# A gated decoder step on one core: longer rows for the activations, and matmuls in passes instead of turns

## The chip, the cores and the metric

The kernel runs on one core of a Trainium2 chip. The metric is the device time of one execution in microseconds. The kernel before was timed three times: 1818.37, 1818.59 and 1819.75 us, median 1818.59. A further execution was taken by the hardware profiler; all rows of profiles below come from such executions. "Before" and "after" are the two kernels.

## What is computed

The reference is one layer of a hybrid decoder for 336 tokens (16 learned meta tokens, 256 of a prompt, 8 sequences of 8), with a model width of 2048. Cut to what matters:

```python
h = rms_norm(x, norm_w)
proj = h @ w_in                       # 2048 -> z | x,B,C | dt | short-conv b,c,h,z | gates a,b
xbc = silu(causal_dwconv(xbc) + b)    # width 4
y, state = ssd_chunked(xs, dt, log_a, bm, cm, state, chunk)
y = gated_group_rms_norm(y + d_skip * xs, z, ssd_norm_w)
y_a = y @ w_ssd_out                   # 4096 -> 2048
u = sc_c * sc_h
y_b = (sc_b * causal_dwconv(u) * silu(sc_z)) @ w_sconv_out
merged = sigmoid(g_a) * y_a + sigmoid(g_b) * y_b
out = rms_norm(x + merged @ w_o, final_norm_w)
```

Nearly all arithmetic is in the matrix products: `w_in` has 176.5 blocks of 128 columns, and the three output products have 64 more of the same size.

## The kernel before, in words

Tokens lie along the free dimension and model channels along the 128 partitions. An activation such as the normalized h is a tile of 16 rows (k = 0 to 15) per partition, each row holding the tokens of one block of 128 channels. A product of 128 output channels is then 16 steps over k: a weight tile of 128x128 is loaded into TensorE and a row of up to 336 tokens is streamed past it, and all steps add up in one PSUM bank.

Accuracy comes from a split. Every operand is kept as a high part (rounded to the float32r type) and a low part (the remainder), and three of the four partial products are added: high weight by high activation, high by low, low by high. The activations' parts are `hhi` and `hlo` (both in the tile `hx`), `vhi` and `vlo` for the short-conv branch, `yh` and `yl` for the SSD branch, and, in the first 80 us, before the norm is known, `uhi` and `ulo`.

`wblk` (lines 92 to 99) brings 1024 columns of weights, that is eight k, by a DMA on SP's queue into `wraw`; ACT copies it to the high part `whi` (L96), and DVE subtracts to get the low part `wlo` (L98). `wraw`, `whi` and `wlo` have three buffers each. `unit` (lines 119 to 124) does two such halves for a product of 2048 channels, each with one call of `mm` (lines 110 to 117), which is where the matmuls are issued: 8 k per call, and in the SSD output (`out_units`) 4 k per call. `proj` is `unit` on h, from token t0 on: t0 is 0 for the x and B channels of the SSD (336 columns), 12 for the C channels and for the short conv's c and h (324), and 16 for the rest (320). The matmuls of dt (L340, L341) and those of the last two blocks of the final product have loops of their own.

A row of `hx` is 352 floats long (TS, 1408 bytes), of which 336 are used; rows of `vhi` and `vlo` are 320 floats (1280 bytes), rows of `yh` and `yl` likewise, and rows of `uhi` and `ulo` 336 floats (1344 bytes).

The order of instructions on each engine is that of the program text, except for a few placed by hand after a named instruction and the SSD's steps, which are woven between the projections of the next group (`weave`). What may run when is set by semaphores that a framework places.

Of the kernel before, what the change touches and what calls it, by code (L numbers as in the profile page):

```python
# [8 lines left out]
F32R = mybir.dt.float32r  # L9
# [3 lines left out]

P = 128
T = 336
TS = 352
META = 16
TC = 12
TV = T - META
DM = 2048  # L20
KT = DM // P
# [28 lines left out]
def tile_hybrid_step(ctx, tc, xT, w0, w1, w2, wdt, wso, wsc, wo, cmask, vec, hvec, convst, sconvst, xe_, fwe, h0T,  # L50
                     yA, yB, yE, convo, ssmp, ssms, sconvo):
    nc = tc.nc
# [19 lines left out]
    xk = xT[:, KT:].rearrange("p (k t) -> p k t", t=T)  # L72
    hx = keep.tile([P, 2, KT, TS], F32R, name="hx")[:, :, :, :T]
    hhi, hlo = hx[:, 0], hx[:, 1]
# [15 lines left out]
    latest = {}  # L90
# [17 lines left out]
                                                                         mybir.DependencyReason.DATA), reason="step")  # L108

    def mm(out, hi, lo, xh, xl, base, nk, k0, first, last):  # L110
        for k in range(nk):
            w = hi[:, base + k * P:base + k * P + P]
            nc.tensor.matmul(out, w, xh(k0 + k), start=first and k == 0, stop=False)  # L113
            nc.tensor.matmul(out, w, xl(k0 + k), start=False, stop=False)  # L114
        for k in range(nk):
            w = lo[:, base + k * P:base + k * P + P]
            latest["pe"] = nc.tensor.matmul(out, w, xh(k0 + k), start=False, stop=last and k == nk - 1).ins  # L117

    def unit(src, xh, xl, n):
        pt = ps.tile([P, 512], F32, name="pj")  # L120
        for half in range(2):
            hi, lo = wblk(src[:, half * 1024:half * 1024 + 1024])
            mm(pt[:, :n], hi, lo, xh, xl, 0, 8, half * 8, half == 0, half == 1)
        return pt[:, :n]
# [47 lines left out]
    with tc.tile_pool(name="pa", bufs=2) as pa:  # L172
# [33 lines left out]
        for k in range(KT):  # L206
            split = nc.scalar.activation(uhi[:, k, :], ya[:, k, :], AF.Copy, scale=yan[:, k:k + 1])
            rest = nc.vector.scalar_tensor_tensor(ulo[:, k, :], ya[:, k, :], yan[:, k:k + 1], fb(uhi[:, k, :]), mult, sub)
            if k % 2 == 0:
                hi = wp.tile([P, 1024], F32R, name="whi")  # L210
                lo = wp.tile([P, 1024], F32R, name="wlo")
# [6 lines left out]
            for i, t0 in enumerate((TC, TC, META)):  # L218
                o = 384 * (k % 2) + i * P
                for j, (w, x) in enumerate(((hi, uhi), (hi, ulo), (lo, uhi))):  # L220
                    nc.tensor.matmul(pu[i][:, :T - t0], w[:, o:o + P], x[:, k, t0:],  # L221
                                     start=k == 0 and j == 0, stop=k == 15 and j == 2)
# [86 lines left out]
            nc.vector.tensor_tensor(up[:, :258], up[:, :258], rs2[:, 14:272], mult)  # L309
            nc.vector.tensor_tensor(ups[:, :, 2:10], ups[:, :, 2:10], eights(rs2[:, 272:]), mult)  # L310

        vhi = pa.tile([P, KT, TV], F32R, name="vhi", bufs=1)
        vlo = pa.tile([P, KT, TV], F32R, name="vlo", bufs=1)
        for j in range(KT):
            u = ((up0, ups0), (up1, ups1), u2)[j] if j < 3 else conv_in(j, proj)
            if j == 3:
# [133 lines left out]
    with tc.tile_pool(name="pb", bufs=2) as pb:  # L450
# [285 lines left out]
        def out_units(g, st):  # L736
            yh, yl = st["y"]
            for mp in range(8):
                hi, lo = wblk(wso[g, mp])
                for i in range(2):  # L740
                    m = 2 * mp + i
                    pp = ps.tile([P, 512], F32, name="pj")
                    mm(pp[:, :TV], hi, lo, lambda k: yh[:, k, :], lambda k: yl[:, k, :], 512 * i, 4, 0, True, True)
                    if g == 0:
                        nc.scalar.activation(ya[:, m, :TV], pp[:, :TV], AF.Copy)
                    else:
                        nc.vector.tensor_tensor(ya[:, m, :TV], ya[:, m, :TV], pp[:, :TV], add)  # L747
                yield
# [59 lines left out]
    with tc.tile_pool(name="pc", bufs=3) as pc_:  # L808
# [42 lines left out]
        for m in range(KE, KT):  # L851
# [3 lines left out]
            for half in range(2):  # L855
# [6 lines left out]
                for wide in ((True, False), (False, True))[half]:  # L862
                    for k in range(8):
                        w, x = (h, hx[:, :, 8 * half + k, :NA]) if wide else (l, hhi[:, 8 * half + k, :NA])
                        nc.tensor.matmul(po[:, :(1 + wide) * NA], w[:, k * P:k * P + P], x,  # L865
                                         start=half + k == 0 and wide, stop=half == 1 and k == 7 and wide)
# [20 lines left out]
        def tokens(a, b):  # L887
            for k in range(a, b):
                x = hx[:, :, k, NA:TV]
                for j, (h, w) in enumerate(((0, eh), (1, eh), (0, el))):  # L890
                    nc.tensor.matmul(pt_, x[:, h, :], w[:, :, k * P:k * P + P], start=k == 0 and j == 0,  # L891
                                     stop=k == KT - 1 and j == 2)
            return nc.cur_bb.bb.instructions[-1]

        first = tokens(0, 4)
# [12 lines left out]
        last = tokens(9, KT)  # L908
# [97 lines left out]
def _build(shapes):  # L1006
    import concourse.bacc as _bacc
    import concourse.tile as _tile

    nc = _bacc.Bacc("TRN2", target_bir_lowering=False, num_devices=1, dynamic_dma_scratch_size=8192)  # L1010
    args = [nc.dram_tensor(n, s, F32, kind="ExternalInput").ap() for n, s in shapes]
    args += [nc.dram_tensor(n, s, F32, kind="ExternalOutput").ap() for n, s in _OUTS]
    with _tile.TileContext(nc) as tc:
        tile_hybrid_step(tc, *args)
    return nc
# [23 lines left out]
```

## Time and profile before

| | before |
|---|---|
| median of three runs (lowest to highest) | 1818.59 us (1818.37 to 1819.75) |
| the profiled execution, its own time | 1817.73 us |
| its span, first to last instruction | 1815.9 us |
| mean granted TensorE clock | 0.999 |
| PE busy | 1808.9 us (100%) |
| DVE busy | 1149.1 us (63%) |
| ACT busy | 830.0 us (46%) |
| POOL busy | 389.7 us (21%) |
| HBM read, written | 296.34 MB, 32.88 MB (181 GB/s) |

PE is TensorE's matmuls, PEld its weight loads, which run beside the matmuls. A matmul lasts some 310 ns from its start to its modelled end, but the next one starts long before that end, so PE reads as busy all the time however dense the matmuls are. What tells how fast they follow each other is the distance between two starts. In the rows, "L117" is a line of the kernel, `pj<-hx,wlo` says that the PSUM tile pj is written from the tiles hx and wlo, and `128x320` is the form of the streamed operand. A group's row ends with its busy time in us, the mean duration of one in ns, and the idle time of its engine before it.

### The profile page before, as it was taken

Reading aid. Unit: us, or ns where it says so; the run is one execution under the profiler, and the core shown is the slowest. Engines: PE = TensorE matmul, PEld = TensorE weight load, DVE = VectorE, ACT = ScalarE, POOL = GpSimd, SP = SyncE. Lnnn points to the kernel's source line nnn. Section 1 sums busy time; section 2 is a strip of 40 time slices with the busy share of each in tenths; the row PEclk is TensorE's granted clock in tenths of the full one; section 3 lists DMA queues with packets and bytes.
Section 4 is the critical chain, followed back from the end, with each engine's and each line's share of the span. In section 5 each row is a group of like instructions: output and inputs, shape, how many; then the busy total and the mean of one; then the engine's idle time right before and its main releaser. Section 6 shows DMA issues by size and latency. Waiting matters only on the chain.

```text
span 1815.9 us, 32410 instructions
## 1 busy us (share of the span) xinstructions
PE 1808.9 (100%) x13006; PEld 1792.9 (99%) x13006; DVE 1149.1 (63%) x1696; ACT 830.0 (46%) x1269; POOL 389.7 (21%) x398
## 2 busy tenths in 40 slices
PE   9999999999999999999999999999999999999998
PEld 9999999999999999999999999999999999999998
DVE  7845544454643335658587786877878778676534
ACT  6433333333333334546655354564546556343543
POOL 0100000000000001243253432524334252400012
PEclk9999999999999999999999999999999999999999
DMA  7444444444444446457566574665746657576553
GB/s 257 144 151 149 148 149 148 151 150 149 154 155 160 161 160 229 151 174 237 169 205 228 172 246 154 209 218 181 247 152 216 205 171 251 157 245 214 181 174 127
DMA packets 117286, 331.33 MB, mean 182 GB/s; under 512 B 20944, under 2 KB 37904, under 8 KB 117136
## 3 DMA queue, kind: packets, MB, share of 16 engines
q1 hardware_dynamic: 116272, 327.89, 55.8%
q8 instruction: 102, 1.67, 0.4%
q10 hardware_dynamic: 864, 1.38, 0.2%
q14 instruction: 48, 0.39, 0.1%
HBM read 296.34 MB, written 32.88 MB: 181 GB/s over the span
## 4 chain that ended last, share of the span: by engine, by line
PE 99%; DMA 0%; issue 0%; DVE 0%; POOLq 0%; POOL 0%; ACT 0%; DVEq 0%
PE pj L113 31%; PE pj L114 31%; PE pj L117 31%; PE yb L653 2%; PE ms L639 1%; PE pj L221 1%; PE yb L588 1%; PE ms L537 1%; PE pj L865 1%; PE ms L221 0%; PE yb L716 0%; PE yb L891 0%; PE ms L540 0%; DMA yan<-xT 0%; PE ms L539 0%; PE pj L340 0%
## 5 line engine op out<-in xcount | busy, mean ns | idle before, releaser
L113 PE MATMUL pj<-hx,whi 128*128 128x320 f32 (+2 forms) x2880 | 860.9, 311 | 0.0
L114 PE MATMUL pj<-hx,whi 128*128 128x320 f32 (+2 forms) x2880 | 856.7, 310 | 0.0
L98 DVE TENSOR_TENSOR wlo<-wraw,whi 128x1024 fp32r<-128x1024 f32 x470 | 599.2, 1275 | 404.7 <-PE pj L117 204.1
L96 ACT ACTIVATE whi<-wraw 128x1024 fp32r<-128x1024 f32 x470 | 496.9, 1058 | 756.7 <-PE pj L114 624.0
L113 PEld LDWEIGHTS pj<-hx,whi 128*128 128x128 f32 x2880 | 540.7, 188 | 4.6 <-ACT pad L465 1.7
L114 PEld LDWEIGHTS pj<-hx,whi 128*128 128x128 f32 x2880 | 540.9, 188 | 0.1
L117 PE MATMUL pj<-hx,wlo 128*128 128x320 f32 (+2 forms) x2880 | 484.6, 310 | 0.0
L117 PEld LDWEIGHTS pj<-hx,wlo 128*128 128x128 f32 x2880 | 440.4, 188 | 0.0
L113 PE MATMUL pj<-yh,whi 128*128 128x320 f32 x512 | 153.1, 311 | 0.0
L114 PE MATMUL pj<-yl,whi 128*128 128x320 f32 x512 | 152.1, 308 | 0.0
L599 POOL TENSOR_TENSOR h<-h,decS 128x512 f32<-128x512 f32 x64 | 76.5, 1230 | 147.4 <-PE ms L639 147.4
L244 POOL COPY SCS<-up 128x2 f32<-128x2 f32 x16 | 21.0, 1310 | 358.3 <-DVE up L238 328.2
L113 PEld LDWEIGHTS pj<-yh,whi 128*128 128x128 f32 x512 | 96.0, 188 | 1.2 <-issue 0.2
L114 PEld LDWEIGHTS pj<-yl,whi 128*128 128x128 f32 x512 | 96.0, 188 | 0.6
L117 PE MATMUL pj<-yh,wlo 128*128 128x320 f32 x512 | 95.8, 309 | 0.0
L747 DVE TENSOR_TENSOR yan<-yan,pj 128x320 f32<-128x320 f32 x112 | 54.2, 485 | 62.6 <-PE pj L117 61.3
L474 DVE SCALAR_TENSOR_TENSOR cacc<-pad,V,cacc 128x360 f32<-128x360 f32 (+1 forms) x144 | 89.5, 621 | 2.0
L467 POOL COPY pad<-cs 128x24 f32<-128x24 f32 x48 | 55.2, 1151 | 127.0 <-DVE cacc L474 114.0
L117 PEld LDWEIGHTS pj<-yh,wlo 128*128 128x128 f32 x512 | 80.3, 188 | 0.0
L114 PE MATMUL pj<-vlo,whi 128*128 128x320 f32 x256 | 75.6, 307 | 0.0
L113 PE MATMUL pj<-vhi,whi 128*128 128x320 f32 x256 | 75.5, 308 | 0.0
L468 POOL COPY cs<-pad 128x3 f32<-128x3 f32 x48 | 45.4, 946 | 79.8 <-ACT pad L465 79.4
(286 smaller groups left out, 1719.8 us busy)
## 6 DMA issues: line engine op xcount, KB each, us to landing
wraw<-w SPq DMA_DIRECT2D x346, 512.0 KB, 3.8
wraw<-wso SPq DMA_DIRECT2D x64, 512.0 KB, 3.6
wraw<-wsc SPq DMA_DIRECT2D x32, 512.0 KB, 3.8
h<-h0T SPq DMA_DIRECT2D x32, 512.0 KB, 5.1
ssms<-h SPq DMA_DIRECT2D x32, 512.0 KB, 4.6
wraw<-wo SPq DMA_DIRECT2D x32, 512.0 KB, 3.8
xq_d<-xe SPq DMA_DIRECT2D x16, 320.0 KB, 3.3
W<-ac_d SPq DMA_DIRECT2D x8, 576.0 KB, 6.6
```

The source lines that it names most:

```text
L96: latest["act"] = nc.scalar.activation(hi[:, :n], raw[:, :n], AF.Copy).ins
L98: latest["dve"] = nc.vector.tensor_tensor(lo[:, :n], raw[:, :n], fb(hi[:, :n]), sub).ins
L113: nc.tensor.matmul(out, w, xh(k0 + k), start=first and k == 0, stop=False)
L114: nc.tensor.matmul(out, w, xl(k0 + k), start=False, stop=False)
L117: latest["pe"] = nc.tensor.matmul(out, w, xh(k0 + k), start=False, stop=last and k == nk - 1).ins
L244: nc.gpsimd.tensor_copy(SCS[:, j, 0, :], up[:, 256:258])
L467: nc.gpsimd.tensor_copy(smp[:, :, 0:3], cs[:, 1:9, :])
L468: nc.gpsimd.tensor_copy(cs[:, 0, :], pad[:, 272:275])
L474: nc.vector.scalar_tensor_tensor(acc[:, i0:], pad[:, i0 + k:360 + k], col(V_CW, 4 * j + k), acc[:, i0:], mult, add)
L599: nc.gpsimd.tensor_tensor(split(h0[b]), split(h0[b]), bc(hv(decS[:, b, :], g), [P, 8, HP]), mult)
L653: nc.tensor.matmul(yb[q * HP:(q + 1) * HP, t, t0:t0 + n], x[:, h * HP:(h + 1) * HP], w[:, h, :], start=i == 0, stop=i == 3)
L747: nc.vector.tensor_tensor(ya[:, m, :TV], ya[:, m, :TV], pp[:, :TV], add)
```

## The change

Three things are edited. `TS` goes from 352 to 368, so rows of `hx` are 1472 bytes long instead of 1408. `vhi` and `vlo` get rows of that length too, of which the first 320 floats are used. And `mm` issues its matmuls in three passes over k: all high by high, then all high by low, then all low by high. Before, high by high and high by low took turns at each k, and low by high came as a pass behind them. The kernel's lines behind `mm` move up by one.

```diff
-TS = 352
+TS = 368
...
     def mm(out, hi, lo, xh, xl, base, nk, k0, first, last):
-        for k in range(nk):
-            w = hi[:, base + k * P:base + k * P + P]
-            nc.tensor.matmul(out, w, xh(k0 + k), start=first and k == 0, stop=False)
-            nc.tensor.matmul(out, w, xl(k0 + k), start=False, stop=False)
-        for k in range(nk):
-            w = lo[:, base + k * P:base + k * P + P]
-            latest["pe"] = nc.tensor.matmul(out, w, xh(k0 + k), start=False, stop=last and k == nk - 1).ins
+        n = 3 * nk
+        for i in range(n):
+            k = i % nk
+            w, x = ((hi, xh), (hi, xl), (lo, xh))[i // nk]
+            latest["pe"] = nc.tensor.matmul(out, w[:, base + k * P:base + k * P + P], x(k0 + k), start=first and i == 0,
+                                            stop=last and i == n - 1).ins
...
-        vhi = pa.tile([P, KT, TV], F32R, name="vhi", bufs=1)
-        vlo = pa.tile([P, KT, TV], F32R, name="vlo", bufs=1)
+        vhi = pa.tile([P, KT, TS], F32R, name="vhi", bufs=1)[:, :, :TV]
+        vlo = pa.tile([P, KT, TS], F32R, name="vlo", bufs=1)[:, :, :TV]
```

On TensorE, at the first product of the short-conv branch (v against `w_sconv_out`, one half of eight k), the order before is:

```order
L117 MATMUL pj<-hx,wlo 128x320 x8
L113 MATMUL pj<-vhi,whi 128x320
L114 MATMUL pj<-vlo,whi 128x320
L113 MATMUL pj<-vhi,whi 128x320
L114 MATMUL pj<-vlo,whi 128x320
...
L117 MATMUL pj<-vhi,wlo 128x320 x8
```

and now:

```order
L115 MATMUL pj<-hx,wlo 128x320 x8
L115 MATMUL pj<-vhi,whi 128x320 x8
L115 MATMUL pj<-vlo,whi 128x320 x8
L115 MATMUL pj<-vhi,wlo 128x320 x8
L115 MATMUL pj<-vhi,whi 128x320 x8
```

The eight matmuls on `vlo` stood between those on `vhi` and now stand behind them; the pass on `wlo` stays third. On TensorE again, in the SSD's stage, where a product of 324 columns is followed by one of 336 columns on h, before:

```order
L117 MATMUL pj<-hx,wlo 128x324 x8
L113 MATMUL pj<-hx,whi 128x336
L114 MATMUL pj<-hx,whi 128x336
L113 MATMUL pj<-hx,whi 128x336
L114 MATMUL pj<-hx,whi 128x336
...
L117 MATMUL pj<-hx,wlo 128x336 x8
```

and now:

```order
L115 MATMUL pj<-hx,wlo 128x324 x8
L115 MATMUL pj<-hx,whi 128x336 x16
L115 MATMUL pj<-hx,wlo 128x336 x8
L115 MATMUL pj<-hx,whi 128x336 x16
L115 MATMUL pj<-hx,wlo 128x336 x8
```

Both parts of h lie in one tile, `hx`, so the two passes on it read as one row of sixteen here: the first eight take `hhi`, the next eight `hlo`. On DVE, ACT, POOL and SP every row stands where it stood. In SBUF, `hx` is 2048 bytes per partition longer and `vhi` and `vlo` 3072 each, and what is allocated behind them lies that much higher.

## The prediction

> **What bounds the kernel now.** I read the page first: busy time, slices, then the chain.
>
> ```profile
> span 1815.9 us, 32410 instructions
> PE 1808.9 (100%) x13006; PEld 1792.9 (99%) x13006; DVE 1149.1 (63%) x1696; ACT 830.0 (46%) x1269; POOL 389.7 (21%) x398
> ...
> PEclk9999999999999999999999999999999999999999
> ...
> PE 99%; DMA 0%; issue 0%; DVE 0%; POOLq 0%; POOL 0%; ACT 0%; DVEq 0%
> PE pj L113 31%; PE pj L114 31%; PE pj L117 31%; PE yb L653 2%; PE ms L639 1%; PE pj L221 1%; PE yb L588 1%; PE ms L537 1%; PE pj L865 1%; PE ms L221 0%; PE yb L716 0%; PE yb L891 0%; PE ms L540 0%; DMA yan<-xT 0%; PE ms L539 0%; PE pj L340 0%
> ```
>
> The chain that ended last is TensorE from end to end, with the full clock granted, and 93% of it lies on the three matmul lines of `mm`, the function that is changed. The waits of PE come next:
>
> ```profile
> PE ms L190 <- DVE warm L175: 1.2, 1, 1.2
> PE pj L830 <- POOL rs_r L826: 0.4, 1, 0.4
> ```
>
> These two are all. No matmul waits for another engine or for a DMA, so the time is a number of matmuls times the distance from one start to the next. A duration on the page is not that distance, because matmuls overlap. The distance comes out in two ways. In the timeline it is the difference of two starts over the matmuls between them. For line 117, whose eight matmuls of a half stand alone in a row, it also comes from the groups by form: busy time over the number of halves is seven distances and one duration.
>
> ```profile
> L117 PE MATMUL pj<-hx,wlo 128*128 128x320 f32 x1696 | 283.0, 308 | 0.0
> L117 PE MATMUL pj<-hx,wlo 128*128 128x336 f32 x640 | 109.1, 313 | 0.0
> L117 PE MATMUL pj<-yh,wlo 128*128 128x320 f32 x512 | 95.8, 309 | 0.0
> L117 PE MATMUL pj<-hx,wlo 128*128 128x324 f32 x544 | 92.5, 311 | 0.0
> L117 PE MATMUL pj<-vhi,wlo 128*128 128x320 f32 x256 | 42.7, 307 | 0.0
> L117 PE MATMUL pj<-uhi,wlo 128*128 128x324 f32 x64 | 10.8, 310 | 0.0
> ```
>
> Lines 113 and 114 have as many matmuls of each form as line 117. Line 117 is already a **pass**: one weight half, eight k in a row. On hx (rows of 1408 bytes) with 320 columns, 1696/8 = 212 halves: (283.0/212 - 0.308)/7 = 146.7 ns. In the same way 324 columns give (92.5/68 - 0.311)/7 = 149.9, and 336 columns (109.1/80 - 0.313)/7 = 150.1. On v (rows of 1280 bytes): (42.7/32 - 0.307)/7 = 146.8; on yh (1280 bytes, four k): (95.8/128 - 0.309)/3 = 146.5; on uhi (1344 bytes), 324 columns: (10.8/8 - 0.310)/7 = 148.6.
>
> Lines 113 and 114 are the **turns**: the same weight tile against xh, then xl. In the timeline of PE, one half each of hx with 320, 324 and 336 columns and of v, first row and the row after sixteen matmuls:
>
> ```profile
> 669.86 0.31 PE L113 MATMUL pj<-hx,whi 128*128 128x320 f32 x1
> ...
> 672.20 1.33 PE L117 MATMUL pj<-hx,wlo 128*128 128x320 f32 x8
> ```
> ```profile
> 329.53 0.31 PE L113 MATMUL pj<-hx,whi 128*128 128x324 f32 x1
> ...
> 331.90 1.36 PE L117 MATMUL pj<-hx,wlo 128*128 128x324 f32 x8
> ```
> ```profile
> 1504.66 0.31 PE L113 MATMUL pj<-hx,whi 128*128 128x336 f32 x1
> ...
> 1507.09 1.36 PE L117 MATMUL pj<-hx,wlo 128*128 128x336 f32 x8
> ```
> ```profile
> 603.04 0.30 PE L113 MATMUL pj<-vhi,whi 128*128 128x320 f32 x1
> ...
> 605.38 1.33 PE L117 MATMUL pj<-vhi,wlo 128*128 128x320 f32 x8
> ```
>
> Turns: 2.34/16 = 146.3 ns (320), 2.37/16 = 148.1 (324), 2.43/16 = 151.9 (336), v 2.34/16 = 146.3. So 324 columns cost less in turns than in a pass, 336 columns less in a pass than in turns, with nothing waiting in either: the distance depends a little on which rows follow each other, and that is all this change can move.
>
> **The change part by part.** Nothing is added or removed: as many matmuls, weight loads, DMAs and vector instructions as before. Weights are loaded afresh for every matmul already, also where the turn keeps them:
>
> ```profile
> L114 PEld LDWEIGHTS pj<-hx,whi 128*128 128x128 f32 x2880 | 540.9, 188 | 0.1
> L113 PEld LDWEIGHTS pj<-hx,whi 128*128 128x128 f32 x2880 | 540.7, 188 | 4.6 <-ACT pad L465 1.7 <-issue 1.2 <-ACT whi L96 0.7
> ```
>
> So giving up the turn loses no reuse. The Trainium skill ("TensorE: Matmul & The Clock Gate", section "Part 2: What happens when you issue a matmul") says that weights can be loaded once for many matmuls, which would speak against parting the two uses of a tile; here 2880 loads for 2880 matmuls on each line show that the turn never used it, and the sum by that rule would be the same.
>
> (1) *Turns into passes.* If every turn takes the distance of today's pass on the same rows: hx 320 columns, 2 x 1696 x (146.7 - 146.3) = +1.4 us; hx 324, 2 x 544 x (149.9 - 148.1) = +2.0; hx 336, 2 x 640 x (150.1 - 151.9) = -2.3; v, 2 x 256 x (146.8 - 146.3) = +0.3; yh, whose rows stay, 0 (the pass, 146.5, is the same distance within rounding). Sum +1.4 us.
>
> (2) *Rows of 1472 bytes* touch all three passes on hx and v. No row of the trace has this pitch. For 320 columns three pitches are seen and all passes take 146.5 to 146.8 (1280 and 1408 above), so I take 146.7 and no gain; the bounds are 149.9 (a pass of 324 columns, +16 us over the 5088 matmuls of hx) and, below, what columns alone cost: the 512-column matmuls
>
> ```profile
> 885.98 0.85 PE L588 MATMUL yb<-xw,bh 128*128 128x512 f32 x3
> 886.66 0.31 PE L113 MATMUL pj<-yh,whi 128*128 128x320 f32 x1
> ```
>
> take 0.68/3 = 227 ns, so (227 - 146.7)/192 = 0.42 ns per column and some 13 ns per matmul besides. For 324 columns the nearest row is uhi, whose pitch like the new one is an odd multiple of 64 bytes: 148.6. I take it for all 1632 matmuls of this form instead of 149.9: -1.3 x 1632 = -2.1 us. Its bounds are 149.9 above and, below, the quickest stretch that the trace has, the first eight matmuls of a half that follows a 336-column one, 1.17/8 = 146.3:
>
> ```profile
> 1474.59 0.31 PE L113 MATMUL pj<-hx,whi 128*128 128x324 f32 x1
> ...
> 1475.76 0.31 PE L113 MATMUL pj<-hx,whi 128*128 128x324 f32 x1
> ```
>
> For 336 columns there is no second pitch. I keep 150.1, the value in a pass; the bounds are 146.3 (a smaller form's best) and the projection of dt, the same rows in turns, (479.56 - 474.61)/32 = 154.7:
>
> ```profile
> 474.61 0.31 PE L340 MATMUL pj<-hx,wd 128*128 128x336 f32 x1
> ...
> 479.56 0.31 PE L113 MATMUL pj<-hx,whi 128*128 128x320 f32 x1
> ```
>
> Over the 1920 matmuls of this form that is -7.3 and +8.8 us about the value taken.
>
> (3) *Who needs what when.* The high weight half is still needed first, the low half still after sixteen matmuls, and both buffers come free at the same matmul; xl is now needed at the ninth matmul instead of the second. The row of L114 loads on hx idles 0.1 us in all, so there is no wait to win. ACT and DVE have room to split the weights:
>
> ```profile
> L98 DVE TENSOR_TENSOR wlo<-wraw,whi 128x1024 fp32r<-128x1024 f32 x470 | 599.2, 1275 | 404.7 <-PE pj L117 204.1
> ```
>
> 1.3 us of every 3.5 us half. If that cover were gone, a late block would cost its own lateness once per half; nothing in the change makes one late. Longer rows shift every later buffer, and the order on DVE, ACT, POOL and SP is the same row for row. Cost 0.
>
> Sum: +1.4 - 2.1 = **-0.7 us** against the profiled execution's own 1817.73 us (span 1815.9 and 1.8 around it). That execution is 0.9 us under the median of the runs, 1818.59; I carry the difference over: 1818.59 - 0.7 = 1817.9, written 1818.
>
> **The rivals.** What this kernel can be told from no change is 0.2%, 3.6 us.
>
> *Faster: the new rows find a better rhythm.* Speaking for it: the same 324-column rows in the same order run at 146.3 in one stretch and at 148.1 in others, so the distance is a matter of how rows fall, not of columns. If 324 columns go from their mean of 148.7 to 146.3 (-3.9 us), 336 from 151.3 down as much (-4.6) and 320 on hx and v by a third of that, 0.8 ns (5856 matmuls, -4.7), the sum is -13 us: 1805. Against it: 320 columns, the largest share, hardly move between three pitches. It decides from 0.4 ns per matmul over the 9408 on hx and v. A stronger form takes the 13 ns beside the columns away from all 9408: -121 us, 1697; no stretch of a half shows it. The Trainium skill (same page, section "Back-to-back issue gap") gives N/2.4 + 2.5 ns for matmuls in a row, 135.8 for 320 columns; the trace disagrees by 11 ns, and by the rule's value the sum would be 9408 x 11 = -103 us, 1715, if row starts were the reason.
>
> *Slower: the 336-column passes fall into the rhythm of the dt projection.* Place: the conv tiles of x and B. Price: 1920 x (154.7 - 151.3) = +6.5 us, with 324 columns at 149.9 (+2.0) and 320 as in (1) (+1.7): +10 us, 1829. For it: with nothing waiting, the same rows show 151.9 and 154.7, so a slow rhythm exists. Against: inside a pass they show 150.1 only. It decides where 336 columns pass 152.4 with the rest as forecast.
>
> *The change does nothing.* The distance follows columns alone and the differences above are chance: 1818.6. It falls inside the forecast.
>
> **How the numbers follow.** No change within 0.2%: 0.46. Faster: 0.36, of which 0.03 for the strong form. Slower: 0.18. The likeliest case's own range is 1815 to 1822. The range of 8 in 10 reaches to the rivals' prices without their far tails: 1803 to 1827.
>
> **What would show it.** Right: in the profile after, one line of `mm` with as many matmuls of each form and no new waits of PE; eight in a row at 146 to 147 ns for 320 columns, 148 to 149 for 324, 150 for 336. Wrong: a distance under 145.5 or over 148 for 320 columns on hx, while yh, whose rows stay, keeps 146.5; or a PE wait on DVE or ACT.

## The result: slower by half a per cent

| | before | after |
|---|---|---|
| median (lowest to highest, four runs each) | 1818.55 us (1818.37 to 1819.75) | 1828.27 us (1828.02 to 1829.54) |
| span of the profiled execution | 1815.9 us | 1826.2 us |
| mean granted TensorE clock | 0.999 | 0.999 |

The ratio is 1.0051, with a 95% interval of 1.0039 to 1.0063. The prediction was 1818 and the top of its range 1827, so it missed on both counts: the change costs 9.7 us.

The profile of after in the order in which that of before was read: from its page the busy time, the granted clock and the chain that ended last.

```profile
span 1826.2 us, 32410 instructions
PE 1819.3 (100%) x13006; PEld 1803.2 (99%) x13006; DVE 1147.8 (63%) x1696; ACT 828.9 (45%) x1269; POOL 390.8 (21%) x398
...
PEclk9999999999999999999999999999999999999999
...
PE 100%; issue 0%; DVE 0%; POOLq 0%; POOL 0%; DVEq 0%
PE pj L115 92%; PE yb L652 2%; PE ms L638 1%; PE pj L220 1%; PE yb L587 1%; PE ms L536 1%; PE pj L864 1%; PE ms L220 0%; PE yb L715 0%; PE yb L890 0%; PE ms L539 0%; PE ms L189 0%; PE ms L538 0%; PE pj L340 0%; PE pj L339 0%; PE ms L700 0%
```

Then the waits of PE in after (line, what it waited for, us in total, times, longest):

```profile
PE ms L189 <- DVE warm L174: 1.2, 1, 1.2
PE pj L829 <- POOL rs_r L825: 0.4, 1, 0.4
```

The instructions are as many as before, on every engine. The waits are the same two, of the same length. DVE, ACT and POOL are busy for the same time within 1.3 us, and TensorE's clock is the same. Only PE's busy time has grown, by 10.4 us, and the span by 10.3. So the matmuls follow each other at a larger distance, and the groups of PE by form in after show on which ones (busy us, mean ns of one):

```profile
L115 PE MATMUL pj<-hx,wlo 128*128 128x320 f32 x1696 | 284.6, 310 | 0.0
...
L115 PE MATMUL pj<-hx,wlo 128*128 128x336 f32 x640 | 111.4, 316 | 0.0
L115 PE MATMUL pj<-yh,whi 128*128 128x320 f32 x512 | 96.8, 311 | 0.0
L115 PE MATMUL pj<-yh,wlo 128*128 128x320 f32 x512 | 95.8, 309 | 0.0
L115 PE MATMUL pj<-hx,wlo 128*128 128x324 f32 x544 | 91.7, 310 | 0.0
...
L115 PE MATMUL pj<-vhi,wlo 128*128 128x320 f32 x256 | 43.0, 310 | 0.0
```

These are the passes that both kernels have, so they compare directly. As in the prediction, busy time over the number of halves is seven distances and one duration. On hx, 320 columns: (284.6/212 - 0.310)/7 = 147.5 ns, against 146.7 before. 336 columns: (111.4/80 - 0.316)/7 = 153.8, against 150.1. 324 columns: (91.7/68 - 0.310)/7 = 148.4, against 149.9. v: (43.0/32 - 0.310)/7 = 147.7, against 146.8. And yh, whose rows stayed, keeps its 95.8 us to the digit. The passes that replaced the turns show the same distances in the timeline of PE in after (start, us, count): three passes over each half of v, one half of hx with 320 columns, and one with 336.

```profile
661.33 1.34 PE L115 MATMUL pj<-vhi,whi 128*128 128x320 f32 x8
...
668.41 2.53 PE L115 MATMUL pj<-hx,whi 128*128 128x320 f32 x16
...
671.96 2.52 PE L115 MATMUL pj<-hx,whi 128*128 128x320 f32 x16
...
1493.69 2.62 PE L115 MATMUL pj<-hx,whi 128*128 128x336 f32 x16
1496.14 1.39 PE L115 MATMUL pj<-hx,wlo 128*128 128x336 f32 x8
```

That is (668.41 - 661.33)/48 = 147.5 ns on v, 3.55/24 = 147.9 on hx, and 2.45/16 = 153.1 for 336 columns.

To see where the 10 us lie, I took the distance of each matmul of `mm` to the next start on PE from the two traces, 11,280 in each, without those above 165 ns (98 before and 97 after, alike in sum, where other work, such as a transpose, or a matmul without a record stands between). The means, in ns, and what the difference makes:

| form | count (whi + wlo) | before, whi / wlo | after, whi / wlo | us |
|---|---|---|---|---|
| hx, 320 columns | 3392 + 1696 | 146.24 / 146.72 | 147.56 / 147.48 | +4.5, +1.3 |
| hx, 324 | 1088 + 544 | 148.18 / 150.00 | 148.32 / 148.36 | +0.2, -0.9 |
| hx, 336 | 1280 + 640 | 151.84 / 150.20 | 153.66 / 153.72 | +2.3, +2.3 |
| v, 320 | 512 + 256 | 146.53 / 146.64 | 147.60 / 147.45 | +0.5, +0.2 |
| yh and yl, 320 | 1024 + 512 | 146.63 / 146.61 | 146.62 / 146.68 | 0, 0 |

The sum is +10.4 us, the whole difference of the spans. What remained to be found out is which of the edits does it, and by what. "Mean distance" below is this figure; it is given as whi / wlo.

### The profile page after: what moved, and what is told of

It is laid out like the page before. It is cut to its first block, busy times and chain, and to the rows that moved or that the text cites. A ratio compares the mean times of both kernels' runs of the same rounds, so it can differ in the third digit from the quotient of the medians.

```text
span 1826.2 us, 32410 instructions
## 1 busy us (share of the span) xinstructions
PE 1819.3 (100%) x13006; PEld 1803.2 (99%) x13006; DVE 1147.8 (63%) x1696; ACT 828.9 (45%) x1269; POOL 390.8 (21%) x398
## 4 chain that ended last, share of the span: by engine, by line
PE 100%; issue 0%; DVE 0%; POOLq 0%; POOL 0%; DVEq 0%
PE pj L115 92%; PE yb L652 2%; PE ms L638 1%; PE pj L220 1%; PE yb L587 1%; PE ms L536 1%; PE pj L864 1%; PE ms L220 0%; PE yb L715 0%; PE yb L890 0%; PE ms L539 0%; PE ms L189 0%; PE ms L538 0%; PE pj L340 0%; PE pj L339 0%; PE ms L700 0%
## 5 line engine op out<-in xcount | busy, mean ns | idle before, releaser
L115 PE MATMUL pj<-hx,whi 128*128 128x320 f32 (+2 forms) x5760 | 921.1, 312 | 0.0
L115 PEld LDWEIGHTS pj<-hx,whi 128*128 128x128 f32 x5760 | 871.0, 188 | 4.7 <-ACT pad L464 1.7
L598 POOL TENSOR_TENSOR h<-h,decS 128x512 f32<-128x512 f32 x64 | 76.5, 1229 | 147.7 <-PE ms L638 147.7
L115 PE MATMUL pj<-yh,whi 128*128 128x320 f32 x512 | 96.8, 311 | 0.0
L115 PE MATMUL pj<-yl,whi 128*128 128x320 f32 x512 | 95.8, 309 | 0.0
L115 PE MATMUL pj<-yh,wlo 128*128 128x320 f32 x512 | 95.8, 309 | 0.0
L115 PEld LDWEIGHTS pj<-yh,whi 128*128 128x128 f32 x512 | 80.5, 188 | 1.9 <-issue 0.2
L115 PEld LDWEIGHTS pj<-yl,whi 128*128 128x128 f32 x512 | 80.3, 188 | 0.0
L846 POOL TENSOR_TENSOR sacc<-sacc,sqf 128x320 f32<-128x320 f32 x13 | 15.3, 1178 | 195.3 <-ACT sqf L844 195.3
L570 POOL TENSOR_TENSOR xe<-xdt,tet 128x512 f32<-128x512 f32 (+1 forms) x24 | 30.3, 1264 | 105.8 <-DVE xdt L541 91.8
L115 PE MATMUL pj<-vhi,whi 128*128 128x320 f32 x256 | 43.0, 310 | 0.0
L115 PE MATMUL pj<-vlo,whi 128*128 128x320 f32 x256 | 43.0, 310 | 0.0
```

The source lines that it names most:

```text
L115: latest["pe"] = nc.tensor.matmul(out, w[:, base + k * P:base + k * P + P], x(k0 + k), start=first and i == 0, stop=last and i == n - 1).ins
L570: nc.gpsimd.tensor_tensor(split(xe[c][:n]), split(xdt[c][:n]), bc(hv(tet[:n, c, :], g), [n, 8, HP]), mult)
L598: nc.gpsimd.tensor_tensor(split(h0[b]), split(h0[b]), bc(hv(decS[:, b, :], g), [P, 8, HP]), mult)
```

## Experiments

All kernels compute the whole reference. Ratios are to the kernel before, run on the same chip beside them, whose median was between 1818.8 and 1819.3 us in each set.

### Which of the edits: one without the other

Three readings stood open. A: the distance depends on the step in memory from one streamed row to the next. B: the passes are slow, whatever the rows. C: longer rows are slow, whatever the order. **passes_1408** is after with the old rows:

```diff
-TS = 368
+TS = 352
...
-        vhi = pa.tile([P, KT, TS], F32R, name="vhi", bufs=1)[:, :, :TV]
+        vhi = pa.tile([P, KT, TV], F32R, name="vhi", bufs=1)
```

(and `vlo` likewise).

> The three passes alone; rows of hx and v as before (1408 and 1280 bytes). Theory A (the distance of two matmuls is set by the step in memory from one streamed row to the next, so each pitch in passes has its own): the distances of the pass of the kernel before hold for all three passes, 146.7 ns for 320 columns, 149.9 for 324, 150.1 for 336: about 1.4 us over before, 1820. Rival B (passes are slow whatever the rows): like the changed kernel, 1828. Rival C (the longer rows are slow whatever the order): like before, 1818.6, with the distances of the turns.

**turns_1472** is before with the new rows: after with the two loops of `mm` as they stood before.

> The rows of 1472 bytes alone, order in turns as before. Its last third is still a pass over rows of 1472 bytes: theory A expects the distances of the changed kernel there (147.5 ns for 320 columns, 153.7 for 336) and others in the turns; if the turns stay as before, (1.3 + 0.2 + 2.2 - 0.9) = 3 us over before, 1821.5. Rival B: as before, 1818.6. Rival C: as the changed kernel, 1828.

passes_1408 took 1819.68 us, ratio 1.0004 [0.9994, 1.0013]: no difference. turns_1472 took 1826.82 us, ratio 1.0042 [1.0027, 1.0057]. So the rows cost about 8 us, and B falls. The passes add 0.7 us on the old rows and some 1.5 on top of the new ones, and the intervals tell neither from nothing. The groups by form of passes_1408:

```profile
L115 PE MATMUL pj<-hx,wlo 128*128 128x320 f32 x1696 | 283.0, 309 | 0.0
L115 PE MATMUL pj<-hx,whi 128*128 128x336 f32 x1280 | 206.7, 314 | 0.0
L115 PE MATMUL pj<-hx,whi 128*128 128x324 f32 x1088 | 174.0, 312 | 0.0
L115 PE MATMUL pj<-hx,wlo 128*128 128x336 f32 x640 | 109.1, 313 | 0.0
```

and of turns_1472, where line 117 is the pass on the low weights:

```profile
L117 PE MATMUL pj<-hx,wlo 128*128 128x320 f32 x1696 | 285.5, 311 | 0.0
...
L117 PE MATMUL pj<-hx,wlo 128*128 128x336 f32 x640 | 110.3, 314 | 0.0
```

In passes_1408 each pass has the distance that the pass of before had on these rows: 320 columns 283.0 us as before, 336 columns 109.1 as before. Its mean distances are 146.63 / 146.59 for 320, 149.84 / 150.00 for 324 and 150.12 / 150.12 for 336, which is part (1) of the prediction's sum almost to the digit. In turns_1472 the 320-column pass on the low weights rises to (285.5/212 - 0.311)/7 = 148.0 ns, although nothing in that pass changed but its rows. Its 336-column pass, (110.3/80 - 0.314)/7 = 152.1 ns, does not show the 153.7 that reading A expected and that after has on the same rows: a first sign that what runs before a pass counts as well.

### Other row lengths

By reading C shorter rows should cost less, and longer ones more. **passes_1344** and **passes_1536** are after with one number changed:

```diff
-TS = 368
+TS = 336     # passes_1344
+TS = 384     # passes_1536
```

> Three passes, rows of hx, vhi and vlo of 1344 bytes (no padding of hx at all). Theory A: another pitch, other distances; the rows of uhi had this pitch in passes in the changed kernel: 145.6 ns for 320 columns and 148.3 for 324. With these and 150 to 154 for 336 columns: 320 columns on hx and v 5856 x -0.8 = -4.7 us, 324 1632 x -0.5 = -0.8, 336 1920 x (-1.3 to +2.4): 1811 to 1818. Rival B: 1828. Rival C: 1818.6 or a little under.

> Three passes, rows of 1536 bytes on hx and v, a multiple of 512, so that every row starts at the same place modulo 512. Theory A: distances of its own, which no row has shown; a spread of 145 to 148 ns for 320 columns is -8 to +9 us: 1810 to 1828. Rival B: 1828. Rival C (longer rows are slower): 1828 or more.

passes_1344: 1819.24 us, 1.0002 [0.9992, 1.0011]. passes_1536: 1828.21 us, 1.0051 [1.0036, 1.0066]. From the groups by form of passes_1344:

```profile
L115 PE MATMUL pj<-hx,wlo 128*128 128x320 f32 x1696 | 281.0, 307 | 0.0
...
L115 PE MATMUL pj<-hx,wlo 128*128 128x336 f32 x640 | 111.8, 317 | 0.0
```

and of passes_1536:

```profile
L115 PE MATMUL pj<-hx,wlo 128*128 128x320 f32 x1696 | 283.2, 309 | 0.0
...
L115 PE MATMUL pj<-hx,wlo 128*128 128x336 f32 x640 | 112.9, 319 | 0.0
```

The two row lengths have opposite effects on the two forms. On rows of 1344 bytes 320 columns are quicker than anything seen before, (281.0/212 - 0.307)/7 = 145.5 ns, while 336 columns stand at (111.8/80 - 0.317)/7 = 154.4. On rows of 1536 bytes 320 columns are back at (283.2/212 - 0.309)/7 = 146.7, and 336 columns are slowest of all, (112.9/80 - 0.319)/7 = 156.0. "Longer is slower" falls: 320 columns are slower at 1472 than at 1536, although the time of passes_1536 is the 1828 that C gave. A was not sharp either: passes_1344 came out 1 us above its 1811 to 1818, with 336 columns at the top of the 150 to 154 ns it allowed for. The next reading to test was the position of one row against the next within a fixed number of bytes.

### The same memory in another order of k

Rows of 1472 bytes are 5 x 256 + 192. Taking k in steps of 3 within a half makes the distance between consecutive rows 3 x 1472 = 17 x 256 + 64, in steps of 5 it is 28 x 256 + 192, and downwards (7 is -1 modulo 8) it is -1472 = -6 x 256 + 64. Eight rows are 46 x 256 bytes, so the steps around the end of a half fit in as well. With this, rows and addresses stay and only the order moves. **k3_1472**, **k5_1472** and **k7_1472** are after with one line changed, and **k3_1408** is passes_1408 with the same line:

```diff
-            k = i % nk
+            k = 3 * i % nk     # k3_1472 and k3_1408; 5 * i in k5_1472, 7 * i in k7_1472
```

If the step counts modulo 256, k3 and k7 must run like rows of 1344 bytes, k5 like after, and k3_1408 (3 x 1408 = 16 x 256 + 128, as 1408 = 5 x 256 + 128) like passes_1408. If it is the length of the rows or their place in memory, all three on rows of 1472 bytes must run like after. The expectations reckoned with the step modulo 512, by which only k3_1472 had a distance already seen; modulo 256 is read off the results.

> The changed kernel with one edit: each pass goes through its eight k in the order 0, 3, 6, 1, 4, 7, 2, 5 instead of 0 to 7 (for the four k of the SSD output 0, 3, 2, 1). Rows stay where they are (1472 bytes), but the step from one streamed row to the next is then 320 modulo 512 bytes at every matmul, as it is with rows of 1344 bytes in plain order. Theory A (the step decides, modulo 512): the distances of the kernel with rows of 1344 bytes come back, 145.5 ns for 320 columns, 148.4 for 324, 154.3 for 336, and its time, 1819. Rival C (the length of the rows or the place where they lie decides): the distances stay 147.5, 148.4 and 153.7, and the time 1828.

> As the run before, with the order 0, 5, 2, 7, 4, 1, 6, 3: steps of 192 modulo 512 bytes, which no kernel so far has. Theory A: distances of its own for each number of columns, somewhere in 145 to 156 ns; nothing finer can be said. Rival C: 147.5, 148.4, 153.7 and 1828.

> As the two runs before, with k downwards (0, 7, 6, ... 1): steps of 64 modulo 512 bytes. Theory A: distances of its own; if only the size of the step counted and not its sign, they would be those of 448: 147.5, 148.4, 153.7. Rival C: 147.5, 148.4, 153.7 and 1828.

> Three passes on rows of 1408 bytes (v 1280 bytes as before the change), k in the order 0, 3, 6, 1, 4, 7, 2, 5: steps on hx of 128 modulo 512 bytes instead of 384. Theory A: the distances on hx leave 146.6, 149.9 and 150.1 ns (320, 324, 336 columns), to values not known; those on v (step 256 either way) stay at 146.6. Rival C: all stay, and the time is that of the passes alone, 1819.7.

| kernel | us | ratio | 320 on hx | 324 | 336 |
|---|---|---|---|---|---|
| k3_1472 | 1820.01 | 1.0006 [0.9997, 1.0016] | 145.80 / 145.69 | 148.38 / 148.32 | 154.22 / 154.35 |
| k7_1472 | 1819.93 | 1.0007 [0.9997, 1.0017] | 145.58 / 145.44 | 148.38 / 148.31 | 154.22 / 154.36 |
| passes_1344 (above) | 1819.24 | 1.0002 [0.9992, 1.0011] | 145.58 / 145.45 | 148.38 / 148.31 | 154.23 / 154.34 |
| k5_1472 | 1828.66 | 1.0056 [1.0041, 1.0071] | 147.56 / 147.47 | 148.33 / 148.33 | 153.67 / 153.70 |
| after | 1828.27 | 1.0051 [1.0039, 1.0063] | 147.56 / 147.48 | 148.32 / 148.36 | 153.66 / 153.72 |
| k3_1408 | 1820.15 | 1.0006 [0.9996, 1.0015] | 146.67 / 146.61 | 149.83 / 150.00 | 150.11 / 150.11 |
| passes_1408 (above) | 1819.68 | 1.0004 [0.9994, 1.0013] | 146.63 / 146.59 | 149.84 / 150.00 | 150.12 / 150.12 |

The groups by form of k3_1472 show it in the profile's own words, in rows that lie where those of after lie:

```profile
L115 PE MATMUL pj<-hx,wlo 128*128 128x320 f32 x1696 | 281.3, 308 | 0.0
...
L115 PE MATMUL pj<-hx,wlo 128*128 128x336 f32 x640 | 111.8, 317 | 0.0
...
L115 PE MATMUL pj<-vhi,wlo 128*128 128x320 f32 x256 | 42.5, 308 | 0.0
```

281.3 us against after's 284.6 for the same matmuls on the same memory. In time the order alone takes the whole loss back. It does so on 320 columns, by 2 ns each, so for these neither the length of the rows nor their place is the cause; 336 columns stay slow in every order on these rows. The means agree within 0.3 ns for the same step modulo 256, while 64 and 192, which are the same modulo 128, differ by 2 ns for 320 columns. And 7 x 1472 and 3 x 1472 differ modulo 512 and agree here; k3_1408, which was expected to change modulo 512, did not. So 256 bytes is the period of these means, as far as multiples of 64 bytes can tell. A part that nobody aimed at fits too: on uhi, with rows of 1344 bytes in all these kernels, a pass of 320 columns on the low weights shows 145.5 ns in ones, 145.6 in fives (step 64), and 147.5 in threes or downwards (step 192).

| step from one streamed row to the next, modulo 256 | seen at | 320 columns | 324 | 336 |
|---|---|---|---|---|
| 0 | rows of 1536; yh at 1280 (320 only) | 146.6 | 148.7 | 155.9 |
| 64 | rows of 1344; 1472 in threes or downwards | 145.5 | 148.35 | 154.3 |
| 128 | rows of 1408, in ones or threes | 146.6 | 149.9 | 150.1 |
| 192 | rows of 1472, in ones or fives | 147.5 | 148.35 | 153.7 |

For 320 columns (1280 bytes, a multiple of 256) the quickest step is 64; for 336 columns (1344 bytes, 64 more) it is 128. In both, the next row then begins 64 bytes, modulo 256, behind the end of the one that is streamed. 324 columns do not follow this.

Two limits of the table. Only 64 and 192 were compared on rows that stay where they are; for 0 and 128 the pitch, and with it the place of the rows, changed too. The loss of 336 columns, from a step of 128 to one of 192, is thus shown for the pitch; that 1344 and 1472 in threes agree to 0.01 ns there speaks for the step, but their place is not excluded. And the means hide a spread: on the last 672 matmuls of 320 columns on hx, the final product, which starts at the first token of a row, a step of 64 gives 145.0 / 145.0 in passes_1344 and 145.1 / 145.1 in k7_1472, but 146.5 / 146.7 in k3_1472.

### Is it the weights?

The weights are loaded for each matmul and lie 512 bytes apart. A rival was that the distance comes from how a weight tile's address stands against the streamed row. **w576** puts the weight tiles of consecutive k 576 bytes apart, so their step is 64 modulo 256; it is after with the following (the two instructions that fill the tiles take the new shape and are left out here):

```diff
-        hi = wp.tile([P, 1024], F32R, name="whi")
...
-        lo = wp.tile([P, 1024], F32R, name="wlo")
...
+        hi, lo = (wp.tile([P, 1152], F32R, name=nm).rearrange("p (k c) -> p k c", c=144)[:, :, :P] for nm in ("whi", "wlo"))
...
-            latest["pe"] = nc.tensor.matmul(out, w[:, base + k * P:base + k * P + P], x(k0 + k), start=first and i == 0,
+            latest["pe"] = nc.tensor.matmul(out, w[:, base // P + k, :], x(k0 + k), start=first and i == 0,
```

and **wshift128** moves all that is allocated behind hx, the weights among it, up by 128 bytes:

```diff
     hx = keep.tile([P, 2, KT, TS], F32R, name="hx")[:, :, :, :T]
     hhi, hlo = hx[:, 0], hx[:, 1]
+    keep.tile([P, 32], F32, name="gapw")
```

> The changed kernel with the split weights of each k 576 bytes apart instead of 512: the weight tiles that are loaded then move by 64 modulo 256 bytes from matmul to matmul. Theory A (only the streamed rows count): 147.5, 148.4 and 153.7 ns, 1828. Rival D (weight load and streamed row disturb each other, and the difference of their two steps decides, 192 - 64 = 128): 146.6, 149.9 and 150.1 ns on hx, 1820.

> The changed kernel with all weight tiles, and everything else behind hx, 128 bytes higher; v moves with the weights, hx does not. Theory A and rival D: nothing changes, 147.5, 148.4 and 153.7 ns, 1828. Rival E (where the weights lie against the rows modulo 256 decides): the distances on hx change and those on v stay.

w576: 1827.18 us, 1.0044 [1.0030, 1.0057]. wshift128: 1828.12 us, 1.0049 [1.0035, 1.0063]. Both stay as slow as after within the intervals; the mean distances are 146.95 / 146.96 and 147.61 / 147.61 for 320 columns on hx, 153.93 / 153.89 and 153.18 / 153.15 for 336. These two moves of the weights shift a form by up to 0.6 ns, but they do not make the 10 us. Moving hx itself, with the rows' steps kept, was not tried.

### Choosing the steps, and a miss

If each form takes the distance of its step, the best kernel gives each form its own: 64 to 320 columns, 128 to 336. **steps_best** has rows of 1344 bytes everywhere, yh and yl too, and takes the 336-column products first over the even k of all three passes, then over the odd ones:

```diff
-TS = 368
+TS = 336
...
-            k = i % nk
-            w, x = ((hi, xh), (hi, xl), (lo, xh))[i // nk]
+            k, p = i % nk, i // nk
+            if out.shape[-1] == T:
+                k, p = 2 * (i % 4) + i // 12, i // 4 % 3
+            w, x = ((hi, xh), (hi, xl), (lo, xh))[p]
...
-                    yh = pb.tile([P, 4, TV], F32R, name="yh", bufs=1)
+                    yh = pb.tile([P, 4, TS], F32R, name="yh", bufs=1)[:, :, :TV]
```

(and `yl` likewise). **turns_part64** asks the same of the turns: before, with 64 bytes between the two parts of hx, so that both steps of a turn are 64 instead of 0 and 128:

```diff
-    hx = keep.tile([P, 2, KT, TS], F32R, name="hx")[:, :, :, :T]
+    hx = keep.tile([P, 2, KT * TS + 16], F32R, name="hx")[:, :, :KT * TS].rearrange("p i (k t) -> p i k t", t=TS)[:, :, :, :T]
```

> Three passes, rows of hx, v and also yh and yl of 1344 bytes, so that the step from row to row is 64 modulo 256 bytes for 320 and 324 columns; products of 336 columns go through the even k of all three passes first and then the odd ones, which makes the step 128 modulo 256 in 22 of 24 matmuls. Theory A (the step modulo 256 decides, and each number of columns has its own best): 145.5 ns for 320 columns on all of hx, v and yh, 148.4 for 324, 150.4 for 336; against before 5088 x -0.9, 768 x -0.7, 1536 x -1.1, 1632 x -0.4 and 1920 x -0.9 ns, together -9 us: 1810. Rival (the pitch of the rows decides, not the order in them): 336 columns stay at 154.3, 1817.

> The kernel before with 64 bytes put between the high and the low part of hx: in the turns both steps, from high to low and on to the next high row, are then 64 modulo 256 bytes instead of 0 and 128 by turns; the pass on the low weights keeps 128. Theory A: in the turns on hx 145.5 ns for 320 columns, 148.4 for 324, 154.3 for 336, in the pass 146.6, 150.0 and 150.1 as before; 3392 x -0.7, 1088 x +0.2, 1280 x +2.5 ns: +1 us, 1820. If the order as such counted, the turns stay at 146.2, 148.2 and 151.8.

Both missed. steps_best took 1820.17 us, 1.0006 [0.9998, 1.0015], where it should have gained. turns_part64 took 1823.60 us, 1.0027 [1.0017, 1.0036]. In steps_best 320 columns do as the table says, 145.65 / 145.53 on hx, and yh comes down from 146.6 to 146.01 / 145.88; but 336 columns, nearly all of whose steps are 128, show 153.94 / 153.59 and not 150.1. In turns_part64 320 columns in turns on hx, all at steps of 64, show 146.76 and not 145.5, and 336 columns 153.77. So the step from the row before is not all that counts. The pass on the low weights in turns_part64 shows it most plainly. Its rows and its steps of 128 are those of the kernel before, where it takes 150.2 ns; here it takes 152.16 in the mean. In the timeline of PE, two of these passes, each with the row that follows:

```profile
712.12 1.41 PE L117 MATMUL pj<-hx,wlo 128*128 128x336 f32 x8
713.37 0.32 PE L113 MATMUL pj<-hx,whi 128*128 128x336 f32 x1
...
719.53 1.36 PE L117 MATMUL pj<-hx,wlo 128*128 128x336 f32 x8
720.74 0.31 PE L113 MATMUL pj<-hx,whi 128*128 128x336 f32 x1
```

Eight matmuls take 1.25 us in the first and 1.21 in the second; by single starts that is 155.6 and 150.0 ns. Of the 80 such passes 43 run at 149.7 to 150.4 and 37 at 153.5 to 155.6, in one kernel, on one tile and with one step. Which it is depends on what came before: all slow ones stand in the first or second half behind products of another form or other work, and from the third half on every pass runs at 150.0.

One more run moves only the step between passes. **passes_part64** is passes_1408 with the 64 bytes between the parts of hx (the line above): inside each pass the step is still 128, and only the step between passes changes, apart from what lies behind hx, which is 128 bytes higher as in wshift128.

> Three passes on rows of 1408 bytes, with 64 bytes put between the high and the low part of hx: all steps inside a pass are still 128 modulo 256 bytes, but the two steps of each half that cross from high to low and back are moved by 64. Theory A as it stood (each step sets the distance by itself): nothing to see beyond 2 of 24 matmuls, 146.6, 149.9 and 150.1 ns on hx and 1820, as the passes alone. Theory A2 (the steps set the rhythms that are possible, and which one runs is carried on from matmul to matmul until a step of another kind throws it over): the 336-column matmuls show the slower rhythm of the run with even and odd k in part, 152 to 156 ns: +3 to +11 us over the passes alone.

It took 1818.32 us, 0.9996 [0.9987, 1.0006], under both expectations. The 336-column matmuls do lose, but the mean distances of 324 columns fall to 148.56 / 147.87, from 149.84 / 150.00 in passes_1408, and that of the 320-column pass on the low weights to 146.08, from 146.59, and give it back: the time is within the interval of passes_1408. Its groups by form:

```profile
L115 PE MATMUL pj<-hx,whi 128*128 128x336 f32 x1280 | 209.6, 316 | 0.0
...
L115 PE MATMUL pj<-hx,wlo 128*128 128x336 f32 x640 | 109.0, 313 | 0.0
```

and two of its halves in the timeline of PE:

```profile
1504.99 2.59 PE L115 MATMUL pj<-hx,whi 128*128 128x336 f32 x16
1507.41 1.36 PE L115 MATMUL pj<-hx,wlo 128*128 128x336 f32 x8
1508.61 2.59 PE L115 MATMUL pj<-hx,whi 128*128 128x336 f32 x16
```

The pass on the low weights keeps its 109 us and 1.20/8 = 150.0 ns. The sixteen on the high weights rise from 206.7 us in passes_1408 to 209.6, and to 2.42/16 = 151.3 ns here against 150.0. By single starts the first eight of this half, on `hhi`, run at 150.0 ns and the second eight, on `hlo`, at 153.2, all with a step of 128 bytes. So it is in all 80 halves for the second eight (153.2 to 154.0), and in 50 of them for the first eight; the other 30 first eights, each in the first half behind products of another form or other work, take 150.6 to 156.9. One form at one step thus has more than one distance. Whether `hlo` is slow for the odd step that leads to it or for its place, 64 bytes off that of `hhi`, this run does not separate. That 336 columns showed 151.9 and 154.7 in the same order on the same rows in the kernel before would fit a dependence on what came before; no run followed it up.

### Putting it to use

Two kernels take, form by form, what had been measured as a whole rather than what the table of steps says. **mix_1408** keeps rows of 1408 bytes on hx and the turns for 320 and 324 columns there, takes the passes for 336 columns, for the first 80 us (uhi) and for v and yh, and gives v, yh and yl rows of 1344 bytes:

```diff
-TS = 368
+TS = 352
...
-            k = i % nk
-            w, x = ((hi, xh), (hi, xl), (lo, xh))[i // nk]
+            k, p = i % nk, i // nk
+            if turns and i < 2 * nk:
+                k, p = i // 2, i % 2
+            w, x = ((hi, xh), (hi, xl), (lo, xh))[p]
...
-        return unit(src, lambda k: hhi[:, k, t0:T], lambda k: hlo[:, k, t0:T], T - t0)
+        return unit(src, lambda k: hhi[:, k, t0:T], lambda k: hlo[:, k, t0:T], T - t0, t0 > 0)
...
-        vhi = pa.tile([P, KT, TS], F32R, name="vhi", bufs=1)[:, :, :TV]
+        vhi = pa.tile([P, KT, T], F32R, name="vhi", bufs=1)[:, :, :TV]
...
-                    yh = pb.tile([P, 4, TV], F32R, name="yh", bufs=1)
+                    yh = pb.tile([P, 4, T], F32R, name="yh", bufs=1)[:, :, :TV]
```

(the final product takes turns as well). **mix_1344** has rows of 1344 bytes everywhere, passes for 320 and 324 columns, and turns over the even k, then the odd k, for 336:

```diff
-TS = 368
+TS = 336
...
-            k = i % nk
-            w, x = ((hi, xh), (hi, xl), (lo, xh))[i // nk]
+            k, p = i % nk, i // nk
+            if out.shape[-1] == T:
+                k, p = (i // 2, i % 2) if i < 16 else (i - 16, 2)
+                k = 2 * (k % 4) + k // 4
+            w, x = ((hi, xh), (hi, xl), (lo, xh))[p]
```

with yh and yl as in steps_best.

> Every form in the quickest place it was seen, on hx rows of 1408 bytes: passes for 336 columns (150.1 ns), turns for 320 and 324 columns on hx as before (146.2 and 148.2), passes with rows of 1344 bytes for v, yh and yl (145.9). Theory A and A2: against before 1280 x -1.7, 768 x -0.7, 1536 x -0.7 ns, together -3.8 us: 1815, if the 336-column passes keep 150.1 behind the turns of their neighbours. Were a neighbour's rhythm carried in: 336 columns at 152 or more, 1818 or more.

> Rows of 1344 bytes on hx, v, yh and yl, passes for 320 and 324 columns as in the run with even and odd k, but turns for 336 columns, over the even k and then the odd ones, so that the steps in a turn are 0 and 128 modulo 256 bytes as before the change. Theory A: 336 columns at 151.8 ns in turns and 152 to 154 in their pass, 320 at 145.6, 324 at 148.4: about -5 us against before, 1814. Theory A2: the same if the rhythm of the turns survives the odd step at each half, 155 ns and 1818 if not.

mix_1408: 1815.10 us, 0.9979 [0.9970, 0.9988]. mix_1344: 1815.24 us, 0.9982 [0.9973, 0.9991]. Both are quicker than before and than after, by about 3.6 and 13 us. From the groups by form of mix_1408:

```profile
L117 PE MATMUL pj<-hx,whi 128*128 128x336 f32 x1280 | 206.7, 314 | 0.0
...
L117 PE MATMUL pj<-yh,wlo 128*128 128x320 f32 x512 | 95.3, 308 | 0.0
...
L117 PE MATMUL pj<-vhi,wlo 128*128 128x320 f32 x256 | 42.3, 307 | 0.0
```

and of mix_1344:

```profile
L118 PE MATMUL pj<-hx,wlo 128*128 128x320 f32 x1696 | 280.8, 307 | 0.0
...
L118 PE MATMUL pj<-hx,wlo 128*128 128x336 f32 x640 | 110.7, 314 | 0.0
...
L118 PE MATMUL pj<-yh,wlo 128*128 128x320 f32 x512 | 95.3, 308 | 0.0
```

They gain in different places. mix_1408 gets v to (42.3/32 - 0.307)/7 = 145.0 ns and yh to (95.3/128 - 0.308)/3 = 145.5 (145.8 in the mean over all its matmuls), and takes 336 columns at 150.1 in all passes; mix_1344 gets 320 columns on hx to (280.8/212 - 0.307)/7 = 145.4 and loses with 336, at 153.48 / 152.73, so the rhythm of the turns did not survive. The 145.0 on v was not foreseen: passes_1344 has the same rows and order on v and shows 145.96 / 145.86, which makes it one more form with two distances at one step. Mean distance times count gives -4.7 us for the first and -3.8 for the second against before; -3.7 and -3.6 were measured.

## Why the prediction was wrong, step by step

**What bounds the kernel: right.** A number of matmuls times a distance. Nothing else moved, and the table of distances accounts for the whole difference.

**(1) Turns into passes, +1.4 us: right.** Alone it measured +0.7 us, with an interval of -1.1 to +2.4 that does not exclude nothing (mean distance times count gives +0.8), and the distances on the old rows came out as taken: 146.6 (taken 146.7), 149.9 (149.9), 150.1 (150.1). A pass on given rows keeps its distance when the two others are made passes too.

**(2) Rows of 1472 bytes, -2.1 us: the step that failed.** Alone they measured +7.9 us in turns (turns_1472), and in passes after stands 8.6 us above passes_1408. The runs' distances say which of the term's three parts failed. For 320 columns the prediction took 146.7 "and no gain", because three pitches had shown the same; it was 147.5 on hx and 147.6 on v, +0.8 ns or more on 5856 matmuls. For 336 columns it kept 150.1 because there was no second pitch; it was 153.7, +3.6 ns on 1920 matmuls. For 324 columns it took 148.6 from uhi, a row whose rounding leaves 0.9 ns either way (the mean there is 148.0), and 148.35 was measured; with a step of 64 on uhi and 192 here, that these two agree is luck. The error was not in a row that was read but in what was carried over: a pitch was treated as a length, and what the runs showed to count, by order alone for 320 columns, is the step to the next row modulo 256 bytes. 1280 and 1408 bytes are steps of 0 and 128, which for 320 columns give the same distance; 1472 bytes is a step of 192, which no pass in the trace of before had. Calling 1344 and 1472 alike as odd multiples of 64 holds for 324 columns only: 64 and 192 are 2 ns apart for 320. Nor could the trace have shown that. Its one pass of 320 columns at a step of 64, 48 matmuls on uhi behind turns, reads 146.8 ns; in the kernels in passes the same matmuls read 145.5.

**(3) Who needs what when, 0: right.** No wait came, and yh, with its rows as they were, kept 146.6, which speaks against a cause that acts on every matmul.

**The slow rival: right in its total by luck, half right in its reason.** It said 1829 and named the place for 336 columns at 154.7; 153.7 and 1828.27 were measured. But of the 10.4 us only 4.6 lie there. 6.5 us come from 320 columns on hx and v, which it counted as +1.7 for the order alone, and 324 columns, which it had at +2.0, gave 0.7 back. Against it the prediction set that inside a pass 336 columns show 150.1 only. That was true of the passes before, whose step is 128. **The fast rival** had the right kind of cause, the way rows fall, with the wrong sign here: the step that gains for 320 columns is reached with rows of 1344 bytes, and with 1472 only in another order of k.

**The range.** Its bounds for part (2) were +16 us for 320 columns and +8.8 for 336; its top, 1827 or some +8.4 us, was said to reach to the rivals' prices, but the slow rival's own 1829 lies outside it; and it left out a loss on 320 and 336 columns at once.

## What to carry to other kernels

When nothing waits and one engine's instructions fill the span, compare distances from start to start by form, since the busy time of overlapping matmuls reads 100% in both a good and a bad rhythm. Before a row pitch is changed, work out the step between consecutively streamed rows for each form and order of k, modulo 256 bytes here, and measure a pitch that has not been run: two pitches that run alike say nothing of a third. One pitch can be right for one width and wrong for another, so the order of k, which is free, is the first thing to try, as it took back 8 us here with the memory untouched.

## What the hardware showed that was not expected

Matmuls of 320 to 336 columns with nothing waiting, at full granted clock, follow each other at mean distances of 145.0 to 156 ns. The order of the same rows moves 320 columns by 2.0 ns (145.5 at a step of 64, 147.5 at 192), 336 by 0.6 (154.3 and 153.7) and 324 by nothing; over all pitches the means of 324 span 1.5 ns and those of 336 5.8 ns (150.1 to 155.9). The Trainium skill ("TensorE: Matmul & The Clock Gate", section "Back-to-back issue gap") gives N/2.4 + 2.5 ns, there for the gap of an isolated matmul, where the prediction took it for matmuls in a row; the estimate by this rule is 135.8 ns for 320 columns and 142.5 for 336. The lowest means here are longer, 145.0 and 150.0, and the rule has no term for an address.

Three things stay open. What inside the chip makes the step count, and why modulo 256 bytes, no run shows: two moves of the weights did not make the difference, and the runs say nothing of what is left. That a form at one step has more than one distance, 150.0 and 153 to 156 for 336 columns at 128, was seen in turns_part64, passes_part64 and steps_best, and not explained; the step alone therefore does not predict a mixed order, as several runs missed by that. And why 324 columns are equally quick at 64 and at 192 was not followed up. A kernel that gives 320 columns a step of 64 and 336 columns an undisturbed 128 was not found; by the table it would take both gains.
